# One triangular-inverse chain for both chunks and both heads of block 2, in place of one chain per chunk

## The chip, the cores and the metric

The kernel runs on one core of a Trainium2 chip. Its engines work side by side, each through its own instructions in order: TensorE (PE, matrix products, with PEld for its weight loads), VectorE (DVE), ScalarE (ACT), GpSimd (POOL) and SyncE (SP), which issues the transfers. The metric is the time of one execution on the device, in microseconds, as the median of three runs. A profiled execution gives the trace from which the rows below are taken.

## The reference

Three transformer blocks follow each other on 256 tokens of width 2048. The change touches the recurrent branch of the second block (RWKV-7, 12 heads of 64, both directions of time), of which this is the core:

```python
for d in range(N_DIR):
    wd = -jax.nn.softplus(-(w0[d] + jnp.tanh(w_in[d]) @ w2[d])) - 0.5
    ad = jax.nn.sigmoid(a0[d] + a_in[d] @ a2[d])
    kd = k * (1.0 + (ad - 1.0) * k_a)
    y_sum = y_sum + rwkv7_scan(r4, wd4, kd4, v4, kk, ad4)   # d = 1: on flipped time
...
def step(S, inp):                                           # one token of rwkv7_scan
    r_t, d_t, k_t, v_t, kk_t, b_t = inp
    sa = jnp.einsum('bhij,bhj->bhi', S, -kk_t)
    S = S * d_t[:, :, None, :] + sa[..., None] * b_t[:, :, None, :] + v_t[..., None] * k_t[:, :, None, :]
    return S, jnp.einsum('bhij,bhj->bhi', S, r_t)
```

The state S is 64 x 64 per head. The kernel computes the scan in two chunks of 128 tokens, and for that it needs, for each chunk and head, the inverse of a 128 x 128 matrix: the identity plus a strictly lower part for one direction of time and a strictly upper part for the other.

## The kernel before

The program is written in Python, one function per stage, and a scheduler of the tile layer then sets each engine's order. So the instructions of stages that don't depend on each other stand mixed in an engine's order, and each engine goes through its own order without overtaking.

Block 2's mixing stage (`block2_mix`) runs six pairs of heads (`rwkv_pair(p)`, p = 0 to 5). In a pair, `shift_mix` makes keys, receptances and values by weight products; `rwkv_setup` and `rwkv_rates` make the decay factors of both directions; `fill()` does cross-attention (pairs 0 and 1) or a group of output products (2 to 5). Then, for each of the two chunks n, `rwkv_gram` makes "gram" tiles: per head seven planes of 128 x 128, copied out of PSUM under a triangular mask (L1272). Plane 0 holds both strict triangles, of which the inverse is wanted. `rwkv_scan` uses the other planes and the inverses for both directions, and `gqa_pair` follows with the pair's share of windowed attention.

`pair_inverse` inverts the matrices of one chunk, two heads at a time. It keeps two tiles, "ylo" and "yup", with two planes for each head: the inverse of the lower part with the transpose of that of the upper part, and the reverse. It doubles the block size level by level, from 1 to 64:

- level 0: the matrix and its transpose (L1342) are put under a level mask into the identity;
- levels 1 to 6: `pt`, the matrix by the lower plane (L1349); z, a copy of the upper planes (L1351), and t, a copy of `pt` out of PSUM (L1352), both by ScalarE; the lower and upper product (L1358, L1359); and the puts of their results into the planes under the level's mask (L1339).

A put is a `copy_predicated` of VectorE. It takes its source in order and writes it "zipped": runs of s = 2^level adjacent elements fall by turns into the one plane and the other:

```python
return bass.AP(v.tensor, v.offset, [v.ap[0], (2 * s, 64 // s), (P + s, 2), (1, s)])
```

The chain of chunk 0 works in PSUM lane A and that of chunk 1 in lane B, two banks each, so both can be under way at once. A lane also names its own buffers: "yloA" and "yloB". Block 1 uses the same function with one head.

The weight products of the whole kernel (`wtiles`, L335 and L339) use a high and a low part of each weight, which ScalarE and VectorE split ahead (L290, L291). They depend on little and so stand between the chain's products as filler: where the chain's next product must wait, TensorE is busy with them as long as there are any before it in its order.

Of the kernel before, what the change touches and what calls it, by code (L numbers as in the profile page):

```python
# [18 lines left out]
P = 128  # L19
T = 256  # L20
# [184 lines left out]
class Core:  # L205
# [821 lines left out]
    def block2_mix(self):  # L1027
# [5 lines left out]
        if "lev" not in self.c:  # L1033
            self.load_mask(self.const, "lev")
# [93 lines left out]
    def rwkv_pair(self, p, finish, fill):  # L1128
# [8 lines left out]
        preps, grams, ups = [], [], []  # L1137
# [9 lines left out]
        fill()  # L1147
        for n in range(2):
            with self.on("AB"[n]):
                g, up = self.rwkv_gram(n, preps)  # L1150
                grams.append(g)
                ups.append(up)
        for d in range(2):
            with self.on("AB"[d]):
                self.rwkv_scan(d, preps[d], grams, ups, vt, ysum)
        return lambda: self.rwkv_end(p, r, v, [q[2] for q in preps], ysum)

    def rwkv_end(self, p, r, v, kds, ysum):
        rg = self.wtile(self.ins["w2_rg"][p], self.hs)
        gate = self.bp.tile([P, T], F32, name=self.uid("rgate"), tag="rgate", bufs=2)  # L1160
        self.wmul(gate, rg, self.rstd)
        self.twice_silu(gate, self.bp.tile([P, T], F32, name=self.uid("rgt"), tag="rgt", bufs=1))
        with self.on("A"):
            self.rwkv_finish(p, r, v, kds, ysum, gate)
# [25 lines left out]
    def rwkv_finish(self, p, r, v, kds, ysum, g):  # L1190
# [18 lines left out]
        y = self.tmp("ry")  # L1209
# [45 lines left out]
    def rwkv_gram(self, n, dirs):  # L1255
        nc, c = self.nc, self.c
        ch = slice(n * P, n * P + P)
        grams = []
        for h in range(2):
            g = self.tmp("gram", (P, 7, P), bufs=2)  # L1260
            nc.gpsimd.memset(g, 0.0)
            grams.append(g)
        for d, (ar, bk, _, _) in enumerate(dirs):
# [5 lines left out]
            for g, pg in zip(grams, pgs):  # L1269
                for j in range(2):  # L1270
                    dst = g[:, 2 + 3 * d:4 + 3 * d] if j else g[:, 0:2 + 3 * d:1 + 3 * d]
                    nc.vector.copy_predicated(dst, mask, pg[:, j * T:j * T + T].rearrange("p (a t) -> p a t", a=2))  # L1272
        _, up = self.pair_inverse([g[:, 0] for g in grams])
        return grams, up

    def rwkv_scan(self, d, prep, grams, ups, vt, ysum):
# [4 lines left out]
        g = {(n, h, j): grams[n][h][:, j + 3 * d] for n in range(2) for h in range(2) for j in (1, 2, 3)}  # L1281
        ys = [[up[:, h, 1 - d] for h in range(2)] for up in ups]
        state = None
        for n in (first, second):
# [25 lines left out]
            if state is None:  # L1310
# [10 lines left out]
                for hs in HALF:  # L1321
                    nc.scalar.activation(state[hs, hs], pS[hs, hs], AF.Copy, scale=carry[hs])

# [373 lines left out]
```

## Time and profile before

| What | Value |
|---|---|
| median of 3 runs | 3600.6 us (3599.87 to 3605.9) |
| the profiled execution: time, span | 3601.28 us, 3599.5 us |
| TensorE, VectorE, ScalarE, GpSimd busy | 98%, 74%, 50%, 2% of the span |
| granted clock of TensorE, mean | 0.993 |
| chain products L1349 in block 2, first to last | from 1503.8 to 2095.9 us of the span |
| pair 3, from its first gram product to the end of its scans | from 1839.6 to 1892.9 us |

The span runs from the first to the last instruction; the time also has what lies around it. TensorE is nearly always busy, so the table's shares say little on a stage: one has to look at the stretches in which the chains run. Matrix products overlap, and their ends are modelled; the distance from start to start says more than a busy time. A product of 32-bit operands is two instructions in a row.

### The profile page before, as it was taken

The numbers are of one execution on the slowest core, as the hardware profiler recorded it, in microseconds if no ns is written. First come the engines' busy times: TensorE is split into PE (matmuls) and PEld (weight loads), VectorE is DVE, ScalarE is ACT, GpSimd is POOL, SyncE is SP. The second block draws the span as 40 slices with busy tenths as digits, with TensorE's granted clock in tenths as the row PEclk, the third lists the DMA queues.
The fourth block names the chain that finished last, engine by engine and source line by source line (L and its number), as shares of the span: only waits on it lengthen the run. The fifth ranks groups of instructions, "written<-read, shape, count | busy, mean of one in ns | idle before, by whom it ended". The sixth has DMA issues, their size and how long they took to land.

```text
span 3599.5 us, 59008 instructions
## 1 busy us (share of the span) xinstructions
PE 3514.4 (98%) x22656; PEld 3144.6 (87%) x22656; DVE 2662.4 (74%) x5500; ACT 1814.2 (50%) x3138; POOL 61.6 (2%) x190
## 2 busy tenths in 40 slices
PE   8889999999999999999999999999999999999998
PEld 6889998999999998888888888889888888888887
DVE  7788988776767668877878867778776666666666
ACT  4156665544545455555555545554444544444444
POOL 0000000000000000000000000000000000000000
PEclk9989999999999999999999999999999999999999
DMA  8965777656666557332234336574445545555554
GB/s 337 351 237 200 263 266 265 225 208 219 222 206 231 188 181 239 133 125 107 103 115 138 125 117 213 188 253 170 172 168 185 187 176 202 176 198 180 195 184 144
DMA packets 128011, 700.99 MB, mean 195 GB/s; under 512 B 14449, under 2 KB 39537, under 8 KB 58865
## 3 DMA queue, kind: packets, MB, share of 16 engines
q1 hardware_dynamic: 127730, 697.22, 55.0%
q8 instruction: 179, 2.93, 0.3%
q14 instruction: 102, 0.84, 0.1%
HBM read 686.94 MB, written 10.22 MB: 194 GB/s over the span
## 4 chain that ended last, share of the span: by engine, by line
PE 86%; DVE 8%; ACT 3%; DMA 1%; issue 1%; SPq 0%; ACTq 0%; DVEq 0%
PE acc L335 36%; PE acc L339 18%; PE acc L309 12%; PE acc L313 6%; DVE wlo L291 2%; DVE ada L496 2%; PE acc L1349 1%; ACT whi L290 1%; PE acc L1358 1%; PE acc L1359 1%; PE acc L623 1%; PE acc L990 1%; PE acc L374 1%; DMA ada<-in_w_ada 1%; PE acc L369 1%
## 5 line engine op out<-in xcount | busy, mean ns | idle before, releaser
L290 ACT CAST whi<-wraw 128x1024 fp32r<-128x1024 f32 x1118 | 1096.1, 982 | 1199.0 <-PE acc L335 706.9
L291 DVE TENSOR_TENSOR wlo<-wraw,whi 128x1024 fp32r<-128x1024 f32 x1118 | 1272.7, 1140 | 514.5 <-ACT whi L290 412.4
L335 PE MATMUL acc<-a,whi 128*128 128x512 f32 x5888 | 1535.6, 396 | 6.7 <-ACT gt L346 1.7
L335 PEld LDWEIGHTS acc<-a,whi 128*128 128x128 f32 x5888 | 1043.1, 188 | 197.9 <-issue 5.4
L339 PEld LDWEIGHTS acc<-a,wlo 128*128 128x128 f32 x5888 | 816.9, 188 | 75.4 <-issue 4.0
L339 PE MATMUL acc<-a,wlo 128*128 128x256 f32 x5888 | 848.7, 282 | 0.0
L309 PE MATMUL acc<-a,whi 128*128 128x258 f32 (+1 forms) x3872 | 523.5, 284 | 0.2 <-ACT whi L290 0.2
L309 PEld LDWEIGHTS acc<-a,whi 128*128 128x128 f32 x3872 | 485.4, 190 | 0.9 <-ACT whi L290 0.4
L313 PE MATMUL acc<-a,wlo 128*128 128x258 f32 (+1 forms) x1936 | 282.8, 284 | 0.0
L313 PEld LDWEIGHTS acc<-a,wlo 128*128 128x128 f32 x1936 | 252.2, 190 | 0.3 <-issue 0.3
L496 DVE SCALAR_TENSOR_TENSOR ada<-ada,csilu 128x2048 f32<-128x2048 f32 x96 | 219.4, 2285 | 9.0 <-DMA ada<-in_w_ada 8.7
L1339 DVE COPY_PREDICATED ylo<-m_lev,acc 128x128 f32<-128x128 uint8 x200 | 82.8, 416 | 48.6 <-PE acc L1359 47.6
L369 PE MATMUL acc<-whi,a 128*128 128x256 f32 x416 | 108.3, 290 | 1.8 <-ACT whi L290 1.8
L1351 ACT COPY z<-yup 128x128 f32<-128x128 f32 x192 | 56.1, 300 | 102.5 <-DVE yup L1339 59.9
L370 PE MATMUL acc<-whi,a 128*128 128x256 f32 x416 | 107.6, 288 | 0.0
L356 DVE TENSOR_TENSOR x<-acc,x 128x256 f32<-128x256 f32 x128 | 54.2, 424 | 51.7 <-PE acc L339 51.7
L347 DVE TENSOR_TENSOR gt<-acc,gt 128x256 f32<-128x256 f32 x214 | 89.0, 418 | 3.5 <-ACT gt L346 2.9
L346 ACT COPY gt<-acc 128x256 f32<-128x256 f32 x214 | 78.0, 364 | 17.6 <-PE acc L339 17.6
L369 PEld LDWEIGHTS acc<-whi,a 128*128 128x128 f32 x416 | 80.0, 192 | 2.8 <-ACT whi L290 2.0
L370 PEld LDWEIGHTS acc<-whi,a 128*128 128x128 f32 x416 | 79.9, 192 | 0.0
L1359 PE MATMUL acc<-z,t 128*128 128x128 f32 x384 | 72.4, 278 | 0.2 <-ACT t L1352 0.2
L1358 PE MATMUL acc<-t,z 128*128 128x128 f32 x336 | 69.2, 290 | 2.0 <-ACT t L1352 2.0
(514 smaller groups left out, 3372.7 us busy)
## 6 DMA issues: line engine op xcount, KB each, us to landing
wraw<-in_w_up SPq DMA_DIRECT2D x132, 1024.0 KB, 4.8
ada<-in_w_ada SPq DMA_DIRECT2D x96, 1024.0 KB, 5.2
wraw<-in_w_down SPq DMA_DIRECT2D x128, 704.0 KB, 4.1
wraw<-in_w_out SPq DMA_DIRECT2D x48, 1024.0 KB, 4.9
wraw<-in_w_mg SPq DMA_DIRECT2D x48, 1024.0 KB, 4.9
wraw<-in_w_gate SPq DMA_DIRECT2D x44, 1024.0 KB, 4.7
wraw<-in_w_rs SPq DMA_DIRECT2D x20, 1024.0 KB, 5.1
wrow<-in_w_rows SPq DMA_DIRECT2D x16, 1024.0 KB, 8.5
```

The costliest lines, as they stand in the source:

```text
L290: nc.scalar.copy(hi[:, :m], raw[:, a:a + m])
L291: nc.vector.tensor_sub(lo[:, :m], raw[:, a:a + m], hi[:, :m].bitcast(F32))
L309: nc.tensor.matmul(acc, w, m, start=(n == 0), stop=False)
L313: nc.tensor.matmul(acc, lo[:, k % 8 * P:k % 8 * P + P], hs[k - c * kt][0], start=False, stop=(n == last))
L335: nc.tensor.matmul(both, hi[:, k % 8 * P:k % 8 * P + P], hs[k - c * kt][2], start=(n == 0), stop=False)
L339: nc.tensor.matmul(acc[:, :T], lo[:, k % 8 * P:k % 8 * P + P], hs[k - c * kt][0], start=False, stop=(n == last))
L347: self.nc.vector.tensor_add(out, acc[0], out)
L369: self.nc.tensor.matmul(accs[t], hs[k][0][:, ts], hi[:, ws], start=(k == 0), stop=False)
L370: self.nc.tensor.matmul(accs[t], hs[k][1][:, ts], hi[:, ws], start=False, stop=False)
L496: nc.vector.scalar_tensor_tensor(raw, raw, 1.0, self.cs, op0=ALU.mult, op1=ALU.mult, accum_out=self.mod[:, n:n + 1])
L1358: nc.tensor.matmul(pu4[:, 0, h], z2[:, h], t1[:, h], start=True, stop=True)
L1359: nc.tensor.matmul(pu4[:, 1, h], t1[:, h], z2[:, h], start=True, stop=True)
```

## The change

`group_inverse` takes the place of the two calls of `pair_inverse` in block 2. One tile "gram" (7 planes x 4 matrices x 128) holds both chunks and both heads. The planes of ylo and yup stand outside and the four matrices inside, so that one instruction handles all four: per level one z, one t, one lower and one upper put, each of 512 columns. The lower and the upper products go into PSUM tiles of their own, `pl` and `pu`, all lower ones first. `load_levels` loads the level masks a second time, at the start of block 2, and casts them into four copies side by side. One memset clears the gram tile. Two scratch tiles ("rgt", "ry") now come from the ring "gt" of six buffers.

```diff
-        if "lev" not in self.c:
-            self.load_mask(self.const, "lev")
+        self.lev4 = self.load_levels(bp, 4)
...
+        grams = self.bp.tile([P, 7, 4, P], F32, name=self.uid("gram"), tag="gram", bufs=1)
+        nc.gpsimd.memset(grams, 0.0)
         for n in range(2):
             with self.on("AB"[n]):
-                g, up = self.rwkv_gram(n, preps)
-                grams.append(g)
-                ups.append(up)
+                self.rwkv_gram(n, preps, grams)
+        _, up = self.group_inverse(grams[:, 0], self.lev4, "AB")
         for d in range(2):
             with self.on("AB"[d]):
-                self.rwkv_scan(d, preps[d], grams, ups, vt, ysum)
+                self.rwkv_scan(d, preps[d], grams, up, vt, ysum)
...
-        self.twice_silu(gate, self.bp.tile([P, T], F32, name=self.uid("rgt"), tag="rgt", bufs=1))
+        self.twice_silu(gate, self.gt())
...
-        y = self.tmp("ry")
+        y = self.gt()
...
-        _, up = self.pair_inverse([g[:, 0] for g in grams])
-        return grams, up
...
+    def load_levels(self, pool, copies):
+        lo, w = CCOL["lev"]
+        t = pool.tile([P, 7, copies, P], U8, name=f"m_lev{copies}")
+        f = self.wp.tile([P, 2048], F32, name=self.uid("mraw"), tag="wraw", bufs=WRAW)
+        self.nc.sync.dma_start(f[:, :w], self.ins["consts"][:, lo:lo + w])
+        f3 = f[:, :w].rearrange("p (l t) -> p l t", l=7)
+        for j in range(copies):
+            self.nc.vector.tensor_copy(t[:, :, j], f3)
+        return t.rearrange("p l h t -> p l (h t)")
+
+    def group_inverse(self, mats, lev, lanes, lower=False):
+        nc = self.nc
+        H = mats.shape[1]
+        with self.on(lanes[0]):
+            lo, up = (self.tmp(n, (P, 2, H, P)) for n in ("ylo", "yup"))
+            t1, z2 = self.tmp("t1", (P, H, P)), self.tmp("z2", (P, H, P))
...
+        def zipped(t, l, h=0, n=H):
+            v, s = t[:, 0, h], 1 << l
+            return bass.AP(v.tensor, v.offset, [v.ap[0], (2 * s, n * 64 // s), (H * P + s, 2), (1, s)])
...
+        put = lambda t, l, src: nc.vector.copy_predicated(zipped(t, l), flat(lev[:, l], l), flat(src, l))
+        heads = [slice(h * P, h * P + P) for h in range(H)]
+        one = lambda t: t.rearrange("p h t -> p (h t)")
+        pn = bank(lanes[0])
+        for h, hc in enumerate(heads):
+            nc.tensor.transpose(pn[:, hc], mats[:, h], self.ident)
+        put(up, 0, one(mats))
+        put(lo, 0, pn)
+        for l in range(1, 7):
+            pt = bank(lanes[1])
+            for h, hc in enumerate(heads):
+                nc.tensor.matmul(flat(pt[:, hc], l), mats[:, h], zipped(lo, l, h, 1), start=True, stop=True)
+            nc.scalar.copy(flat(one(z2), l), zipped(up, l))
+            nc.scalar.copy(one(t1), pt)
+            both = l < 6 or lower
+            pl = bank(lanes[0]) if both else None
+            if both:
+                for h, hc in enumerate(heads):
+                    nc.tensor.matmul(pl[:, hc], z2[:, h], t1[:, h], start=True, stop=True)
+                put(lo, l, pl)
+            pu = bank(lanes[1])
+            for h, hc in enumerate(heads):
+                nc.tensor.matmul(pu[:, hc], t1[:, h], z2[:, h], start=True, stop=True)
+            put(up, l, pu)
+        return lo, up
```

In the changed kernel the transposes are L1352, the products `pt`, `pl` and `pu` are L1358, L1365 and L1369, z and t are L1359 and L1360, the puts L1347, and the gram products L1262.

Where the program stands on the engines is set by the scheduler. First TensorE in pair 3, ahead of the first chain product. Before, from the first transpose (L1342; `acc_20502` is filler, 20154 and 20156 are the two heads of chunk 0):

```order
L1342 MATMUL acc_20184<-c_ident,gram_20154 128x128
L335 MATMUL acc_20502<-a_15632,whi_20494 128x512
L335 MATMUL acc_20502<-a_15635,whi_20494 128x512
L1342 MATMUL acc_20184<-c_ident,gram_20156 128x128
L335 MATMUL acc_20502<-a_15638,whi_20494 128x512
L335 MATMUL acc_20502<-a_15641,whi_20494 128x512
L335 MATMUL acc_20502<-a_15644,whi_20494 128x512
L1349 MATMUL acc_20191<-ylo_20178,gram_20154 128x128
L335 MATMUL acc_20502<-a_15647,whi_20494 128x512
L1349 MATMUL acc_20191<-ylo_20178,gram_20156 128x128
```

The changed kernel there, from the last gram products (chunk 1, backward) on; ahead of them stand two transposes with two L335 before the first, one between them and five behind:

```order
L1262 MATMUL acc_19944<-ar_19644,bk_19645 128x256 x2
L1262 MATMUL acc_19945<-ar_19644,bk_19645 128x256 x2
L1352 MATMUL acc_19960<-c_ident,gram_19912 128x128
L339 MATMUL acc_20177<-a_15632,wlo_20170 128x256
...
L1352 MATMUL acc_19960<-c_ident,gram_19912 128x128
L339 MATMUL acc_20177<-a_15644,wlo_20170 128x256
...
L335 MATMUL acc_20177<-a_15656,whi_20173 128x512
...
L335 MATMUL acc_20177<-a_15668,whi_20173 128x512
L1358 MATMUL acc_19967<-ylo_19954,gram_19912 128x128 x4
```

Left out are two, then three more L339 of the first and second four and three L335 of the five. The first chain product has moved behind all gram products of the pair, and eight L339 and five L335 stand behind the last of them.

Then the levels on TensorE, pair 3, before (chunk 0's chain reads t_3520, chunk 1's t_3543):

```order
L1349 MATMUL acc_20236<-ylo_20178,gram_20154 128x128
L1358 MATMUL acc_20320<-t_3543_20303,z_3544_20304 128x128
L1349 MATMUL acc_20236<-ylo_20178,gram_20156 128x128
L1359 MATMUL acc_20320<-z_3544_20304,t_3543_20303 128x128
L1358 MATMUL acc_20320<-t_3543_20303,z_3544_20304 128x128
L1359 MATMUL acc_20320<-z_3544_20304,t_3543_20303 128x128
L1358 MATMUL acc_20242<-t_3520_20180,z_3521_20181 128x128
L1359 MATMUL acc_20242<-z_3521_20181,t_3520_20180 128x128
```

and in the changed kernel, levels 2 and 3:

```order
L1365 MATMUL acc_19993<-t_3479_19956,z_3480_19957 128x128 x4
L1369 MATMUL acc_19999<-z_3480_19957,t_3479_19956 128x128 x4
L1358 MATMUL acc_20005<-ylo_19954,gram_19912 128x128 x4
L335 MATMUL acc_20306<-a_15635,whi_20298 128x512
L335 MATMUL acc_20306<-a_15638,whi_20298 128x512
L1452 MATMUL acc_20216<-gt_20210,c_perm 128x256
L335 MATMUL acc_20306<-a_15641,whi_20298 128x512
L335 MATMUL acc_20306<-a_15644,whi_20298 128x512
L1365 MATMUL acc_20012<-t_3479_19956,z_3480_19957 128x128 x4
```

Where one chain's products stood among the other's, four products of one chain now stand in a run, with filler only between `pt` and `pl`. Between these two stand, in pair 3, at level 1 three L335 and one L339; at level 2 seven L339 and one L335; at level 3 the rows above; at level 4 two small products (L1499) and three score products of 64 rows (L1468), with a fourth ahead of the next `pt`; at level 5 three L335 and two L339; at level 6, ahead of `pu`, two L1282 of the scan, three L339 and four transposes.

Last VectorE, pair 3 of the changed kernel, at the first puts and at level 4:

```order
L1268 COPY_PREDICATED gram_19912<-m_tri_b,acc_19944 128x2x128 x2
L1268 COPY_PREDICATED gram_19912<-m_tri_b,acc_19945 128x2x128 x2
L1347 COPY_PREDICATED yup_19955<-m_lev_15744,gram_19912 128x256x2
L1347 COPY_PREDICATED ylo_19954<-m_lev_15744,acc_19960 128x256x2
L291 TENSOR_TENSOR wlo_20303<-wraw_20296,whi_20302 128x1024
...
L1347 COPY_PREDICATED yup_19955<-m_lev_15744,acc_20018 128x32x2x8
L1501 TENSOR_SCALAR hm_20225<-acc_20222 128x4
...
L1504 TENSOR_SCALAR rq_20227<-rq_20227 128x4
L1474 SCALAR_TENSOR_TENSOR sm_20247<-acc_20241,rq_20227,c_win 128x256
L1347 COPY_PREDICATED ylo_19954<-m_lev_15744,acc_20031 128x16x2x16
```

Before, eight puts of 128 columns took the place of the first two here, in groups of four for each chunk, and the small operations of the attention's scale (L1452 to L1455 before, L1501 to L1504 now, twelve in all) had four puts of chunk 1 among them.

## Rows read from the trace of the kernel before

**Rows 1.** The page: busy time by engine, and the chain that ended last.

```profile
PE 3514.4 (98%) x22656; PEld 3144.6 (87%) x22656; DVE 2662.4 (74%) x5500; ACT 1814.2 (50%) x3138; POOL 61.6 (2%) x190
PE 86%; DVE 8%; ACT 3%; DMA 1%; issue 1%; SPq 0%; ACTq 0%; DVEq 0%
```

**Rows 2.** A window of pair 3: length, busy time by engine (instructions), clock, DMA.

```profile
1839.00:1860.00 21.00, 19.63 (x110) 14.38 (x109) 17.70 (x44) 7.83 (x18) 0.00 (x0) 1.00 0.34 118
```

**Rows 3.** TensorE's timeline, filler: start us, length us, engine, line, operation, tiles, count.

```profile
1487.53 2.02 PE L335 MATMUL acc<-a,whi 128*128 128x512 f32 x8
1489.38 1.10 PE L339 MATMUL acc<-a,wlo 128*128 128x256 f32 x8
```

**Rows 4.** TensorE's timeline, pair 3; in brackets idle before, and what ended it.

```profile
1845.90 2.74 PE L1267 MATMUL acc<-ar,bk 64*128 64x256 f32 x16
...
1849.38 0.30 PE L1342 MATMUL acc<-c_ident,gram 128*128 128x128 f32 x1 [0.75 <-DVE gram L1272]
...
1850.02 0.94 PE L335 MATMUL acc<-a,whi 128*128 128x512 f32 x3
1851.15 0.51 PE L1349 MATMUL acc<-ylo,gram 128*128 128x128 f32 x2 [0.20 <-DVE ylo L1339]
1851.40 0.49 PE L335 MATMUL acc<-a,whi 128*128 128x512 f32 x1
1852.27 0.51 PE L1349 MATMUL acc<-ylo,gram 128*128 128x128 f32 x2 [0.39 <-DVE ylo L1339]
...
1854.34 0.39 PE L1358 MATMUL acc<-t,z 128*128 128x128 f32 x2
1854.57 0.39 PE L1359 MATMUL acc<-z,t 128*128 128x128 f32 x2
...
1861.61 0.72 PE L335 MATMUL acc<-a,whi 128*128 128x512 f32 x2
1862.39 0.49 PE L1349 MATMUL acc<-ylo,gram 128*128 128x128 f32 x2
...
1882.62 0.94 PE L335 MATMUL acc<-a,whi 128*128 128x512 f32 x3
1883.68 0.66 PE L1296 MATMUL acc<-xw,yup 128*128 128x64 f32 x4
```

**Rows 5.** VectorE's timeline in pair 3, level 0 and level 1.

```profile
1848.80 1.11 DVE L1272 COPY_PREDICATED gram<-m_tri_b,acc 128x256 f32<-128x256 uint8 x3
...
1851.27 0.95 DVE L1339 COPY_PREDICATED ylo<-m_lev,acc 128x128 f32<-128x128 uint8 x1
1851.84 1.65 DVE L1272 COPY_PREDICATED gram<-m_tri_f,acc 128x256 f32<-128x256 uint8 x4
...
1855.24 0.47 DVE L1339 COPY_PREDICATED yup<-m_lev,acc 128x128 f32<-128x128 uint8 x1
```

**Rows 6.** Line 1339, all instructions: count, shortest/median/longest ns, first and last start.

```profile
L1339 DVE COPY_PREDICATED yup<-m_lev,acc x192: 283/296/504, 239.4 to 2098.2; 128x128 f32<-128x128 uint8 x192
L1339 DVE COPY_PREDICATED yup<-m_lev,gram x24: 714/741/971, 1502.3 to 2074.6; 128x128 f32<-128x128 uint8 x24
```

**Rows 7.** Groups by line: count, busy us, mean ns, idle before and releaser.

```profile
L1272 DVE COPY_PREDICATED gram<-m_tri_b,acc 128x256 f32<-128x256 uint8 x48 | 19.0, 441 | 1.5 <-PE acc L1267 1.5
L1468 ACT COPY sm<-acc 128x512 f32<-128x512 f32 x16 | 9.4, 585 | 8.7 <-PE acc L1466 8.6
```

**Rows 8.** VectorE's timeline, pair 3: first and last operation of the attention's scale.

```profile
1878.67 0.16 DVE L1452 TENSOR_SCALAR hm<-acc 128x4 f32<-128x4 f32 x1
...
1882.65 0.17 DVE L1455 TENSOR_SCALAR rq<-rq 128x4 f32<-128x4 f32 x1
```

**Rows 9.** ScalarE's and TensorE's timelines at the blocks' seam; the mask's cast.

```profile
1431.89 1.05 ACT L290 CAST whi<-wraw 128x1024 fp32r<-128x1024 f32 x1 [1.53 <-DMA wraw<-in_w_rs]
...
1437.19 2.70 PE L335 MATMUL acc<-a,whi 128*128 128x512 f32 x11
...
L242 DVE CAST m_lev<-mraw x1: 621/621/621, 82.0 to 82.0; 128x896 uint8<-128x896 f32 x1
```

More of the change, by code (lines that the diff above doesn't have):

```diff
@@ L1136, in rwkv_pair @@
             kk, vt, ysum = self.rwkv_setup(p, k, v)
-        preps, grams, ups = [], [], []
+        preps = []
         pls = [[], []]
@@ L1253, in rwkv_rates, with rwkv_gram @@
         return ar, bk, kd, carry
-    def rwkv_gram(self, n, dirs):
+    def rwkv_gram(self, n, dirs, grams):
         nc, c = self.nc, self.c
         ch = slice(n * P, n * P + P)
[L1258 to L1262, printed above, removed]
         for d, (ar, bk, _, _) in enumerate(dirs):
@@ L1268, in rwkv_gram @@
             mask = c["tri_b" if d else "tri_f"].rearrange("p (a t) -> p a t", a=2)
-            for g, pg in zip(grams, pgs):
+            for h, pg in enumerate(pgs):
+                g = grams[:, :, 2 * n + h]
                 for j in range(2):
@@ L1272, in rwkv_gram, with rwkv_scan @@
                     nc.vector.copy_predicated(dst, mask, pg[:, j * T:j * T + T].rearrange("p (a t) -> p a t", a=2))
[L1273 to L1276 removed]
+    def rwkv_scan(self, d, prep, grams, up, vt, ysum):
         nc = self.nc
@@ L1280, in rwkv_scan @@
         first, second = (1, 0) if d else (0, 1)
-        g = {(n, h, j): grams[n][h][:, j + 3 * d] for n in range(2) for h in range(2) for j in (1, 2, 3)}
-        ys = [[up[:, h, 1 - d] for h in range(2)] for up in ups]
+        g = {(n, h, j): grams[:, j + 3 * d, 2 * n + h] for n in range(2) for h in range(2) for j in (1, 2, 3)}
+        ys = [[up[:, 1 - d, 2 * n + h] for h in range(2)] for n in range(2)]
         state = None
@@ new lines, in group_inverse, with bank @@
+    def group_inverse(self, mats, lev, lanes, lower=False):
[4 more added lines that the diff above has]
+            t1, z2 = self.tmp("t1", (P, H, P)), self.tmp("z2", (P, H, P))
+        for t in (lo, up):
+            nc.gpsimd.tensor_copy(t.rearrange("p y h t -> p (y h) t"),
+                                  self.ident.unsqueeze(1).to_broadcast([P, 2 * H, P]))
+        def zipped(t, l, h=0, n=H):
+            v, s = t[:, 0, h], 1 << l
+            return bass.AP(v.tensor, v.offset, [v.ap[0], (2 * s, n * 64 // s), (H * P + s, 2), (1, s)])
+        def bank(lane):
+            with self.on(lane):
+                return self.psum(False)[:, :H * P]
+        flat = lambda ap, l: ap.rearrange("p (m e s) -> p m e s", e=2, s=1 << l)
+        put = lambda t, l, src: nc.vector.copy_predicated(zipped(t, l), flat(lev[:, l], l), flat(src, l))
[23 more added lines that the diff above has]
+        return lo, up
```

## The prediction

> **What bounds the kernel now.** I read the page first. TensorE is busy 98% of the span, VectorE 74%, ScalarE 50%, GpSimd 2%, and 86% of the chain that ended last is TensorE [rows 1]. So a microsecond counts only where TensorE stands still or is given more to do. The matrix products of the changed kernel are the same ones: per pair four transposes and 68 chain products, before and after. What can change is how long TensorE waits for the chain, in six places, one per pair.
>
> Then the windows of pair 3, whose stretch from the first gram product to the end of the scans runs from 1839 to 1893 us. In the first 21 us TensorE is idle 1.37 us at full granted clock, while VectorE is busy 17.7 [rows 2]. Pairs 2 to 5 stand in the same order, so pair 3 speaks for them; pairs 0 and 1 have other filler and nearly the same places.
>
> Then TensorE's timeline there. It is in-order, and between chain products stand weight products as filler. Filler back to back starts every 0.23 us (L335: 8 in 1.85 us) and about 0.12 us (L339: 8 in 1.10 us with the last one's tail) [rows 3]; chain products start 0.23 us apart, and a result is out 0.39 us after its start [rows 4]. Against these prices the losses in pair 3 are: 0.75 us ahead of the first transpose; three L335 (0.69) that fill 1.13 us before the first L1349, so 0.44; one L335 (0.23) that fills 0.87 before the second, so 0.64; two L335 (0.46) that fill 0.78, so 0.32; and, at the scan, three L335 that fill 1.06, so 0.37 [rows 4]. That is 1.8 us at the front (level 0), 0.3 in the levels, 0.4 in the scans: 2.5 us per pair, 15 us in all six. More than this, and some small change of switching, the change cannot take away.
>
> **The price of a put.** VectorE's masked write into the zipped planes (L1339) takes 0.30 us for one matrix of 128 columns in most levels and 0.74 at level 0 [rows 6]; at level 1, 0.47, and at level 0 they follow each other every 0.57, so that 0.17 of each is overlapped [rows 5]. The run of adjacent elements is 1 at level 0, 2 at level 1, 4 or more later: the price is by short runs, not by the instruction. A masked copy of 256 columns with long runs takes 0.44 [rows 7], 0.14 more than 128 columns. So my estimates for four matrices in one put: 0.30 + 3 x 0.14 = 0.73 us at levels 2 to 6; 4 x 0.30 + 0.17 = 1.37 at level 1; 4 x 0.57 + 0.17 = 2.45 at level 0. No row shows a hop between planes of 513 elements (it was 129), so for levels 0 and 1 the lower bound is 0.73, as if short runs cost nothing, and the upper the figures given. I take the upper, nearest to the level-0 row, which is the same write with fewer runs.
>
> **The change, part by part.**
>
> *Level 0.* Before, chain 0 begins when chunk 0's grams are masked, at 1849.91 [rows 5], and its first product needs one head's two puts. Now all four matrices of both chunks must be masked, and then two puts of 2.45 us run one after the other. From 1848.63, where TensorE ran dry, the new order gives it, up to the first chain product: 13 L335 (3.0), 8 L339 (0.95), 4 transposes (0.9) and 4 gram products (8 in 2.74 us [rows 4], so 1.4): 6.25 us, plus some 0.4 of waiting at the first two transposes (two L335 now stand ahead of them). It is ready at 1855.3. VectorE masks the forward half of chunk 1 in 1.65 us [rows 5], to 1851.5. The backward half waits for the four gram products, which TensorE reaches at 1851.3 and ends at 1852.7; the last copy is done at 1853.2. Then up to 1855.5 the first put holds VectorE, and the second is done at 1857.95. TensorE waits from 1855.3 to 1858.0, 2.7 us. Front: 0.4 + 2.7 = 3.1 for 1.8 before, **+1.3 us** a pair. With puts at the lower bound there is no wait: 0.4 for 1.8, -1.4.
>
> *Between pl and the next pt.* The split of the PSUM tile lets the lower put run beside the upper products. From the last pl product TensorE has 0.23 + 4 x 0.23 = 1.15 us of work; the put needs 0.39 + 0.73 + about 0.1, a tenth more. Such tenths I take as equal on both sides. At level 1 it needs 0.39 + 1.37 + 0.1, so 0.7 us of wait.
>
> *Between pt and pl.* The chain now has nothing beside it but filler. z and t are 512 columns each; a ScalarE copy of 512 columns takes 0.585 [rows 7]. Upper put, z, then t end about 2.2 us after the first pt product, which covers 0.92 itself: 1.25 us of filler is wanted, and the order has 0.81, 1.06, 1.41, 1.3, 0.93 and 1.7 in the six levels. At level 1 z is done early and 0.1 is short; at level 2 the level-1 puts are late and 0.35 is short; at level 5, 0.3. Sum 0.75.
>
> *VectorE's queue at level 4.* The order puts the attention's 12 small operations and a 128x256 one ahead of the lower put. In the trace such a run takes 4.15 us with four puts and a sum among it [rows 8], about 3.0 without. The put starts some 1.0 us late; a leftover score product covers half: 0.5 us.
>
> Levels: 0.7 + 0.75 + 0.5 = 1.95 for 0.3 before, **+1.6**; if everything were covered, -0.3.
>
> *What comes back.* Both scan directions now start together and fill each other's gaps, so I count the scan's 0.37 as gone. The gram products stand in five groups instead of six, and chain products in runs of four. No row prices a switch alone; it is between nothing and 1.0 us per pair, and I take 0.5. **-0.9**.
>
> *Edits costed at nothing.* The removed instructions on VectorE (52 puts become 13) and ScalarE (36 copies become 12) are off the path here: their engines have idle time in this stretch. The one big memset and the copies of the identity run on GpSimd, 2% busy [rows 1], after the previous pair's scans and some 50 us ahead of use; uncovered they would cost their length, some 3.4 us a pair (four memsets). The two tiles that move to the "gt" ring share six buffers whose other users are done within a few us; uncovered, one transfer each, some 2 us. The new mask is one more load of 0.46 MB ahead of block 2's first weights and four casts of 0.62 us [rows 9] at the seam of the blocks. The first weights were cast from 1431.89 and first used three L335 after 1437.19, at 1437.9 [rows 9]: some 4.9 us of cover after the cast, against a load that is about 3 us later. Uncovered: 2.5 us once.
>
> **Sum.** 1.3 + 1.6 - 0.9 = +2.0 us per pair, +12 in six. The profiled execution took 3601.3 us with a span of 3599.5, 0.7 above the median of 3600.6; its own time plus 12 gives 3613, against the median 3612.6. I say **3612 us**.
>
> **The rivals.** A change under 0.2%, 7 us, is no more than a measurement of this kernel can tell from none.
>
> *A. As above*, 3612. For it: puts priced by runs, and an order whose filler ahead of the first product ends 2.7 us early. Chance 0.42; it decides only while the two level-0 puts together are longer than some 2.2 us.
>
> *B. The level-0 put is cheap with the longer hop.* Then the front is -1.4 and the pair -1.4 + 1.6 - 0.9 = -0.7: 3597. Against it speaks that the price falls only with run length in the rows. [...] Chance 0.18.
>
> *C. Faster.* The one chain is covered everywhere: front -1.4, levels -0.3, the rest -0.9, so -2.6 per pair, 3585. It needs cheap short runs and, in each level, filler that is longer than the order shows. For it: ScalarE and VectorE lose two thirds of the instructions, so everything queued behind them comes earlier. [...] Chance 0.10.
>
> *D. Much slower.* Every level waits as level 4 does, because attention work, weight splits and casts of 1 us stand between the puts in the same queues, and no second chain is there to take TensorE's time: 0.7 us more in each of six levels, +4 a pair, 3636. Chance 0.10.
>
> *E. No change.* The waits are as small as before and only elsewhere: 3601. For it: equal products, and only 15 us of waits to move. Chance 0.20.
>
> Faster by over 0.2%: C and the low end of B, 0.14. Slower: D and most of A, 0.46. Within: 0.40. Case A alone is 3606 to 3619, by the bounds of the levels and the switching. The range takes in B and stops short of C and D, 2 in 10 together: 3590 to 3628.
>
> **What would show it.** In pair 3 after: the first L1358 group ahead of which TensorE idles 2 us or more, released by the lower plane's put; that put at 2.2 to 2.5 us for level 0, 1.3 to 1.4 for level 1, 0.7 later; a wait of about 0.7 ahead of the second L1358 group. Wrong would be: level-0 puts near 1 us (B), no wait ahead of the first group (B, C), waits ahead of every L1365 group (D). TensorE's products must be as many as before, and the seam at 1430 to 1450 without a new wait; a wait there of over 1 us would be a price that I set at nothing.

## The result: slower, 3626.8 us

| | median us | runs | range us |
|---|---|---|---|
| before, in the first comparison | 3600.23 | 4 | 3596.29 to 3605.90 |
| changed | 3626.82 | 4 | 3623.09 to 3628.99 |

The ratio is 1.0076, with a 95% interval of 1.0064 to 1.0088: 26.6 us slower. That is the forecast side, and 3626.8 lies just inside the forecast range (3590 to 3628), but it is more than twice the 12 us of the sum.

The page of the changed kernel, to hold against [rows 1]: as many products on TensorE, fewer operations on the other engines, and yet more of the chain on VectorE (10% for 8).

```profile
PE 3515.8 (97%) x22656; PEld 3145.2 (87%) x22656; DVE 2664.3 (74%) x5270; ACT 1790.5 (49%) x2994; POOL 58.2 (2%) x160
PE 83%; DVE 10%; ACT 3%; issue 2%; DMA 1%; SPq 0%; ACTq 0%; DVEq 0%
```

One full period, from the first gram product of a pair to that of the next, holds all work of a pair. Windows of pair 3 before (columns as in [rows 2]: length, busy time by engine, clock, DMA):

```profile
1839.62:1947.14 107.52, 105.82 (x656) 88.65 (x655) 86.39 (x237) 56.54 (x128) 6.41 (x16) 1.00 0.34 116
```

and of the changed kernel: pair 2, pair 3, 4 us around the first chain product of each, and the 2 us behind that of pair 3.

```profile
1729.21:1840.37 111.16, 105.82 (x655) 88.42 (x655) 85.65 (x198) 52.54 (x105) 6.07 (x11) 1.00 0.33 112
1840.37:1952.87 112.50, 107.18 (x655) 89.73 (x655) 85.63 (x198) 52.54 (x105) 6.07 (x11) 0.98 0.33 110
1754.00:1758.00 4.00, 2.30 (x15) 2.03 (x16) 2.70 (x2) 1.01 (x3) 0.00 (x0) 1.00 0.19 25
1866.00:1870.00 4.00, 3.11 (x11) 2.87 (x12) 1.89 (x2) 0.59 (x1) 0.00 (x0) 0.59 0.26 47
1867.00:1869.00 2.00, 2.00 (x9) 2.00 (x10) 0.89 (x1) 0.00 (x0) 0.00 (x0) 0.50 0.29 41
```

Read them as length less busy. TensorE stood idle 1.70 us in the period of before and 5.32 in pair 3 after: 3.62 more. Its busy time also grew by 1.36 for the same products, with a granted clock of 0.98: from 1867 to 1869 the clock stood at 0.50 of full. In pair 2 the same wait left it at 1.00 and the products took 105.82. Together +5.0 us in pair 3.

Where the idle time stands is in TensorE's timeline of pair 3 (start, length, what; in brackets idle before and its releaser), beside [rows 4]. A count is of instructions, two for a chain or gram product and one for a transpose or a filler product:

```profile
1857.95 0.30 PE L1352 MATMUL acc<-c_ident,gram 128*128 128x128 f32 x1 [0.50 <-DVE gram L1268]
...
1861.35 0.33 PE L1352 MATMUL acc<-c_ident,gram 128*128 128x128 f32 x1 [0.32 <-DVE gram L1268]
...
1866.89 2.08 PE L1358 MATMUL acc<-ylo,gram 128*128 128x128 f32 x8 [2.92 <-DVE ylo L1347]
1868.62 1.63 PE L335 MATMUL acc<-a,whi 128*128 128x512 f32 x3
1870.04 0.33 PE L339 MATMUL acc<-a,wlo 128*128 128x256 f32 x1
1870.21 1.05 PE L1365 MATMUL acc<-t,z 128*128 128x128 f32 x8
...
1872.63 1.16 PE L1358 MATMUL acc<-ylo,gram 128*128 128x128 f32 x8 [0.48 <-DVE ylo L1347]
...
1886.65 1.16 PE L1358 MATMUL acc<-ylo,gram 128*128 128x128 f32 x8 [0.20 <-DVE ylo L1347]
...
1893.15 0.44 PE L1515 MATMUL acc<-c_ident,sm 128*128 128x128 f32 x2 [0.45 <-DVE sm L1513]
```

With 0.41 ahead of the next pair's first gram product (released by VectorE's L1251) these are 5.28 of the 5.32. The same place in pair 2:

```profile
1755.70 1.23 PE L1358 MATMUL acc<-ylo,gram 128*128 128x128 f32 x8 [2.92 <-DVE ylo L1347]
...
1757.61 1.16 PE L1365 MATMUL acc<-t,z 128*128 128x128 f32 x8
```

In pair 2, at full clock, the first chain products and the same four filler products go from 1755.70 to 1757.61, 1.91 us; in pair 3 from 1866.89 to 1870.21, 3.32; in pairs 4 and 5 it is 3.36 and 3.33, and the clock stands at 0.50 in the 2 us behind each of the three waits. So the halved clock costs 1.4 us behind the wait, in pairs 3 to 5. Pairs 0 and 1, with other filler, wait 3.05 and 2.64 us ahead of their first chain products, also at full clock (1.00 in the 2 us behind them); pairs 2 to 5 wait 2.92.

VectorE's timeline shows what was waited for; the puts are L1347:

```profile
1862.19 2.44 DVE L1347 COPY_PREDICATED yup<-m_lev,gram 128x512 f32<-128x512 uint8 x1
1864.27 2.56 DVE L1347 COPY_PREDICATED ylo<-m_lev,acc 128x512 f32<-128x512 uint8 x1
...
1871.30 1.28 DVE L1347 COPY_PREDICATED ylo<-m_lev,acc 128x512 f32<-128x512 uint8 x1 [3.42 <-PE acc L1365]
...
1876.10 0.73 DVE L1347 COPY_PREDICATED ylo<-m_lev,acc 128x512 f32<-128x512 uint8 x1 [0.16 <-PE acc L1365]
```

Level 0, 1 and 2: 2.44, 1.28, 0.73 us, near the estimates of 2.45, 1.37 and 0.73.

Last, the seam of blocks 1 and 2. Rows of filler on TensorE, before; the first and the last correspond to the first and the last of the changed kernel:

```profile
1430.55 2.01 PE L335 MATMUL acc<-a,whi 128*128 128x512 f32 x8
...
1434.40 2.01 PE L335 MATMUL acc<-a,whi 128*128 128x512 f32 x8
...
1449.53 2.01 PE L335 MATMUL acc<-a,whi 128*128 128x512 f32 x8
```

and the changed kernel's, with the wait between them, and below it all four casts of the mask on VectorE (count, shortest/median/longest ns, first and last start):

```profile
1426.46 2.01 PE L335 MATMUL acc<-a,whi 128*128 128x512 f32 x8
...
1432.47 3.16 PE L335 MATMUL acc<-a,whi 128*128 128x512 f32 x8 [2.00 <-ACT whi L290]
...
1449.22 2.01 PE L335 MATMUL acc<-a,whi 128*128 128x512 f32 x8
```

```profile
L1325 DVE CAST m_lev<-mraw x4: 1082/1085/1087, 1427.3 to 1431.3; 128x896 uint8<-128x896 f32 x4
```

Ahead of the seam this execution was 4.1 us earlier than that of before, for reasons that lie before block 2, and behind the seam 0.3 us earlier: 3.8 lost, 2.0 as a wait for block 2's first weights and about 1.1 in eight products at a lowered clock (3.16 us for 2.01, with 0.62 granted from 1432.40 to 1435.70). From the first gram product of pair 0 (1493.20 before, 1492.45 after) to corresponding rows behind the sixth pair (2171.66 before, 2193.64 after) the pairs take 22.7 us more, 3.8 each. The 3.8 at the seam and the 22.7 in the pairs, 26.5 us in these two traces, stand beside the 26.6 of the medians.

### The profile page after: what moved, and what is told of

It reads as the page before. It is cut to its first block, busy times and chain, and to the rows that moved or that the text cites. A ratio compares the mean times of both kernels' runs of the same rounds, so it can differ in the third digit from the quotient of the medians.

```text
span 3621.2 us, 58466 instructions
## 1 busy us (share of the span) xinstructions
PE 3515.8 (97%) x22656; PEld 3145.2 (87%) x22656; DVE 2664.3 (74%) x5270; ACT 1790.5 (49%) x2994; POOL 58.2 (2%) x160
## 3 DMA queue, kind: packets, MB, share of 16 engines
q8 instruction: 178, 2.92, 0.3%
## 4 chain that ended last, share of the span: by engine, by line
PE 83%; DVE 10%; ACT 3%; issue 2%; DMA 1%; SPq 0%; ACTq 0%; DVEq 0%
PE acc L335 35%; PE acc L339 18%; PE acc L309 11%; PE acc L313 6%; DVE wlo L291 2%; DVE ada L496 2%; ACT whi L290 1%; PE acc L623 1%; PE acc L1358 1%; PE acc L990 1%; PE acc L374 1%; PE acc L369 1%; PE acc L370 1%; DMA ada<-in_w_ada 1%; DVE ylo L1347 1%
## 5 line engine op out<-in xcount | busy, mean ns | idle before, releaser
L291 DVE TENSOR_TENSOR wlo<-wraw,whi 128x1024 fp32r<-128x1024 f32 x1118 | 1275.5, 1143 | 514.8 <-ACT whi L290 414.4
L335 PE MATMUL acc<-a,whi 128*128 128x512 f32 x5888 | 1534.8, 396 | 9.1 <-DVE a L391 2.2
L335 PEld LDWEIGHTS acc<-a,whi 128*128 128x128 f32 x5888 | 1044.6, 188 | 204.9 <-issue 8.6
L339 PEld LDWEIGHTS acc<-a,wlo 128*128 128x128 f32 x5888 | 816.4, 188 | 72.8 <-issue 0.7
L339 PE MATMUL acc<-a,wlo 128*128 128x256 f32 x5888 | 840.6, 281 | 0.0
L356 DVE TENSOR_TENSOR x<-acc,x 128x256 f32<-128x256 f32 x128 | 54.2, 424 | 51.6 <-PE acc L339 51.5
L374 PE MATMUL acc<-wlo,a 128*128 128x256 f32 x416 | 70.1, 287 | 0.4 <-DVE wlo L291 0.4
L1358 PE MATMUL acc<-ylo,gram 128*128 128x128 f32 x288 | 44.7, 300 | 20.7 <-DVE ylo L1347 17.6
L357 DVE TENSOR_TENSOR x<-acc,x 128x256 f32<-128x256 f32 x144 | 60.9, 423 | 3.7
L1358 PEld LDWEIGHTS acc<-ylo,gram 128*128 128x128 f32 x288 | 37.5, 202 | 28.8 <-DVE ylo L1347 23.0
```

The source lines that it names most:

```text
L291: nc.vector.tensor_sub(lo[:, :m], raw[:, a:a + m], hi[:, :m].bitcast(F32))
L335: nc.tensor.matmul(both, hi[:, k % 8 * P:k % 8 * P + P], hs[k - c * kt][2], start=(n == 0), stop=False)
L339: nc.tensor.matmul(acc[:, :T], lo[:, k % 8 * P:k % 8 * P + P], hs[k - c * kt][0], start=False, stop=(n == last))
L374: self.nc.tensor.matmul(accs[t], hs[k][0][:, ts], lo[:, ws], start=False, stop=(k == nk - 1))
L1358: nc.tensor.matmul(flat(pt[:, hc], l), mats[:, h], zipped(lo, l, h, 1), start=True, stop=True)
```

## The experiments

All medians stand beside runs of the kernel before on the same chip (3598.9 to 3600.3). Where kernels of different chips are compared, the differences below are taken of what each has over before on its own chip.

**1. Two wide chains.** One `group_inverse` for each chunk:

```diff
-                self.rwkv_gram(n, preps, grams)
-        _, up = self.group_inverse(grams[:, 0], self.lev4, "AB")
+                self.rwkv_gram(n, preps, grams)
+                ups.append(self.group_inverse(grams[:, 0, 2 * n:2 * n + 2], self.lev4, "AB"[n] * 2)[1])
```

> The changed kernel, but with one chain per chunk again: group_inverse is called for the two matrices of chunk 0 right after its grams, in lane A, and for those of chunk 1 in lane B. All else stays: the one gram tile, the planes outside, the products in tiles of their own, the second mask load. Theory (the merging of the chunks costs: TensorE must wait for all grams and for 5 us of level-0 puts, and then runs at half clock): the six pairs come back to what they were, about 22 us less, and the 4 us at the seam of the blocks stay: 3605 us, and no wait of more than 1 us ahead of a first chain product. Rival (the layout with far planes, or the split tiles, or the two small tiles in the other ring cost): little comes back, 3620 us or more.

Measured 3620.79 us, ratio 1.0060 (1.0047 to 1.0073). The theory fell: only 6 us came back. Its timeline of pair 3 still waits for puts, and for the attention:

```profile
1862.48 0.75 PE L1358 MATMUL acc<-ylo,gram 128*128 128x128 f32 x4 [1.10 <-DVE ylo L1347]
...
1869.82 1.19 PE L1358 MATMUL acc<-ylo,gram 128*128 128x128 f32 x8 [0.83 <-DVE ylo L1347]
...
1909.78 0.70 PE L1515 MATMUL acc<-c_ident,sm 128*128 128x128 f32 x4 [1.14 <-DVE sm L1513]
```

So the merging of the chunks is not by itself what costs.

**2. The lower put first.**

```diff
-        put(up, 0, one(mats))
         put(lo, 0, pn)
+        put(up, 0, one(mats))
```

> The changed kernel with the two level-0 puts in the other order, the lower plane first. The first chain product needs only the lower one; z needs the upper one. Theory (the series of the two puts is the wait): the first product starts about 2 us earlier and ScalarE's copy z is waited for instead, about 0.6 us less per pair where the clock stayed up and 2.1 where it fell, about 8 us in six pairs: 3618 us. Rival (the waits in the levels, where one chain has nothing beside it, are the cost): the wait only moves from the first product to the second group, 3627 us.

Measured 3625.15 us, 1.0073 (1.0059 to 1.0087): 1.7 less, nearer to the rival. The first wait fell, but a wait for ScalarE's copies took its place (z waits for the upper put, and t, which the row names, is copied behind z), and another came ahead of the attention's transposes:

```profile
1869.18 1.23 PE L1358 MATMUL acc<-ylo,gram 128*128 128x128 f32 x8 [1.33 <-DVE ylo L1347]
1872.69 1.16 PE L1365 MATMUL acc<-t,z 128*128 128x128 f32 x8 [1.35 <-ACT t L1360]
...
1911.01 0.44 PE L1515 MATMUL acc<-c_ident,sm 128*128 128x128 f32 x2 [2.03 <-DVE sm L1513]
```

**3. Useless work in the wait.**

```diff
             pt = bank(lanes[1])
+            if l == 1:
+                for h in range(8):
+                    nc.tensor.matmul(pt[:, heads[h % 4]], self.ident, up[:, 0, h % 4], start=True, stop=True)
```

> The changed kernel with useless work: eight products of 128 columns (1.8 us of TensorE per pair) that need only the upper level-0 put and whose result is overwritten by the first chain products. They fall in the 2.9 us in which TensorE stands still. Theory (the granted clock falls to half because TensorE stands still that long, and the 1.6 us lost behind the wait in pairs 3 to 5 are that clock's): the clock stays at 1.00 there, and the added work makes the kernel 5 to 9 us faster: 3618 to 3622 us. Rival (the slow products behind the wait have another cause, or the clock falls anyway): not faster, 3627 us, and up to 11 us more where the added products are not hidden.

Measured 3620.63 us, 1.0058 (1.0045 to 1.0070): 6.2 less, with 48 more products. Pair 3, with the added ones as L1359 and the first chain products as L1361, and the clock in the window around them:

```profile
1868.44 2.02 PE L1359 MATMUL acc<-yup,c_ident 128*128 128x128 f32 x16 [1.46 <-DVE yup L1347]
1870.61 1.23 PE L1361 MATMUL acc<-ylo,gram 128*128 128x128 f32 x8
```

```profile
1867.00:1874.00 7.00, 5.42 (x41) 4.99 (x42) 4.89 (x4) 1.26 (x2) 0.00 (x0) 1.00 0.20 43
```

The first chain products take 1.23 us as in pair 2, not 2.08, and the clock stays at 1.00, here and over the periods of pairs 2 and 3 below. So the clock does not fall behind a wait of 1.46 us that ends in the useless products. Not all of the 6 us is the clock's, though. The periods of pairs 2 and 3:

```profile
1733.80:1844.10 110.30, 106.99 (x670) 90.33 (x670) 86.12 (x198) 52.29 (x105) 6.03 (x11) 1.00 0.33 113
1844.10:1954.28 110.18, 106.85 (x671) 90.31 (x671) 86.13 (x198) 52.21 (x105) 6.03 (x11) 1.00 0.33 113
```

Pair 3 takes 2.3 us less than in the changed kernel, but pair 2, where the clock had not fallen, also takes 0.9 less: the order behind the added products is another, and the waits of 0.20 and 0.45 us are gone. That leaves about 1.4 us for the clock in pair 3, and, as an estimate, as much in pairs 4 and 5: some 4 of the 6 us.

**4. No second load of the mask.**

```diff
-        f = self.wp.tile([P, 2048], F32, name=self.uid("mraw"), tag="wraw", bufs=WRAW)
-        self.nc.sync.dma_start(f[:, :w], self.ins["consts"][:, lo:lo + w])
-        f3 = f[:, :w].rearrange("p (l t) -> p l t", l=7)
+        f3 = self.c["lev"].rearrange("p (l t) -> p l t", l=7)
         for j in range(copies):
-            self.nc.vector.tensor_copy(t[:, :, j], f3)
+            self.nc.gpsimd.tensor_copy(t[:, :, j], f3)
```

> The changed kernel without the second load of the level mask: its four copies are made by GpSimd from the mask that block 1 already holds, so no transfer, no buffer of the weights' ring and no VectorE cast at the seam. Theory (the load and its casts hold up the first weights of block 2, 2 us of wait and then half clock): 4 us less, 3623 us, and the wait for the first weights at the start of block 2 is gone. Rival (the seam's loss comes from elsewhere, as from the buffers that the blocks change): 3627 us with the wait still there.

Measured 3626.62 us, 1.0077 (1.0064 to 1.0089): no gain in the median. The wait for the first weights is gone in the trace; one of 1.02 us ahead of L438, for VectorE's L430, stands a little later, and the pairs of this execution took some 3 us more, with the clock lowered in pairs 1 and 2 too (0.76 from 1645 to 1649 us, 0.83 from 1755 to 1765). The wait itself is the load's: all six traces with the load have it (1.67 to 2.14 us), none of the eight without it. The lowered clock behind it shows in two of the six (the next eight L335 take 3.16 us in the changed kernel and 3.61 in 3, 2.12 or 2.13 in the others), and a wait at L438 of about 1.1 us also in 5, where the seam is that of before. In the median the seam's price stays unproven (and see 9).

**5. Before, with the two ring edits alone.**

```diff
-        self.twice_silu(gate, self.bp.tile([P, T], F32, name=self.uid("rgt"), tag="rgt", bufs=1))
+        self.twice_silu(gate, self.gt())
...
-        y = self.tmp("ry")
+        y = self.gt()
```

> The kernel before with one part of the change alone: the two small tiles (rgt, ry) come from the ring of six buffers. Theory (these two edits cost nothing, as forecast): 3600 us. Rival (the shared ring delays the pair's end and is what stays, some 2.5 us per pair, after the chains were separated again): 3612 us or more.

Measured 3603.08 us, 1.0008 (1.0000 to 1.0017). Neither end is excluded: nothing, or some 6 us. The trace shows the 0.42 us ahead of the first gram product that the changed kernel has and before has not, in pairs 2 to 5, 1.7 us in all; the wait ahead of the first transpose falls from 0.75 to 0.50 in return. Pair 3's period is 108.10 us for 107.52, with less idle (1.54 for 1.70) and more busy time. What makes the busy time longer was not traced.

**6. The old chains in the new frame.** `pair_inverse` again for each chunk, on the one gram tile, no second load:

```diff
-        self.lev4 = self.load_levels(bp, 4)
...
-        _, up = self.group_inverse(grams[:, 0], self.lev4, "AB")
+                ups.append(self.pair_inverse([grams[:, 0, 2 * n + h] for h in range(2)])[1])
```

> The changed kernel with the old chains: one gram tile, one memset and the shared ring as in the changed kernel, but pair_inverse for each chunk, one put for each matrix, both products in one PSUM tile, and the old mask without a second load. Theory (what the separated wide chains still had over the kernel before, 3 us at the seam and about 2.5 per pair, comes from the wide instructions, the split tiles and the load): 3601 us. Rival (it comes from the frame: one gram tile, one memset, the ring): 3612 to 3616 us.

Measured 3609.27 us, 1.0029 (1.0018 to 1.0041), between the two. Ahead of its first chain products TensorE waits as in [rows 4]; what is new in pair 3's period is 1.18 us ahead of the attention's transposes, for VectorE's L1512 (1.2 to 1.6 in pairs 1 to 4, 5.2 in all), and 0.42 at the first gram product. So by the medians some 6 us beyond the ring come with the frame. Why the order puts the attention later there was not tried.

**7. A put twice.** One more `put(lo, 0, pn)` behind the two.

> The changed kernel with one suspected cost doubled: the lower level-0 put is written twice (same result). Theory (what VectorE does ahead of the first chain product is TensorE's wait, one for one): 2.4 us more per pair, and half clock behind the wait in more pairs: 3641 to 3646 us. Rival (the levels behind are what costs, and the front is half covered): 3632 us or less.

Measured 3639.59 us, 1.0113 (1.0100 to 1.0127): 14.1 more, 2.3 a pair, about the theory's 2.4 (the time is 1.4 us under its span) and far from the rival. Pair 3:

```profile
1882.06 2.04 PE L1359 MATMUL acc<-ylo,gram 128*128 128x128 f32 x8 [4.60 <-DVE ylo L1347]
```

The wait grew by 1.68: the third put takes 2.34 us and a weight split (L291) of 1.45 now stands ahead of it, but 1.9 us more of filler cover them. The clock now falls in pair 2 too (0.57 from 1765 to 1770 us), which is part of the price.

**8. Level 0 in two plain steps.**

```diff
-        put(up, 0, one(mats))
-        put(lo, 0, pn)
+        def put0(t, tmp, src):
+            v = t[:, 0, 0]
+            zv = bass.AP(v.tensor, v.offset, [v.ap[0], (P, H), (2, P // 2), (H * P + 1, 2)])
+            nc.vector.tensor_mul(one(tmp), src, lev[:, 0])
+            nc.vector.tensor_add(zv, tmp.rearrange("p h (m e) -> p h m e", e=2), zv)
+        put0(up, z2, one(mats))
+        put0(lo, t1, pn)
```

> The changed kernel with level 0 written in two plain steps in place of each predicated put: the matrices times the mask into a scratch tile (512 adjacent columns), then a sum of it with the planes, written zipped with the same far hop. Theory (the predicated write is dear at short runs, not the hop): product and sum some 0.7 us each, the level takes 2.8 instead of 4.9 us of VectorE, the wait ahead of the first product falls under 1 us and the clock stays up: 2 to 4 us less per pair, 3605 to 3613 us. Rival (each write of single elements with a far hop costs the same, predicated or not): the sum takes 2.4 us, the level 6 us, 3633 us or more.

Measured 3603.30 us, 1.0014 (1.0005 to 1.0023): 22.2 of the 26.6 us are back. VectorE, then TensorE in pair 3:

```profile
1855.65 0.68 DVE L1356 TENSOR_TENSOR z<-gram,m_lev 128x512 f32<-128x512 f32 x1
1856.25 0.68 DVE L1356 TENSOR_TENSOR t<-acc,m_lev 128x512 f32<-128x512 f32 x1
1856.85 1.13 DVE L1357 TENSOR_TENSOR yup<-z,yup 128x512 f32<-128x512 f32 x1
1857.82 1.15 DVE L1357 TENSOR_TENSOR ylo<-t,ylo 128x512 f32<-128x512 f32 x1
```

```profile
1856.12 2.01 PE L335 MATMUL acc<-a,whi 128*128 128x512 f32 x8
1857.96 0.64 PE L339 MATMUL acc<-a,wlo 128*128 128x256 f32 x4
1859.12 1.20 PE L1363 MATMUL acc<-ylo,gram 128*128 128x128 f32 x8 [0.53 <-DVE ylo L1357]
```

The level now takes 3.3 us of VectorE (1855.65 to 1858.97) for 4.6 (1862.19 to 1866.83). The rest of the gain has two sources: the order puts eight L335 and four L339 ahead of the first product where five L335 stood, 1.2 us more cover, and the clock stays up (1.00 from 1858 to 1861 us). The period is 108.28 us with 2.56 idle.

**9. The same, without the second load.** Edits 8 and 4 together.

> The changed kernel with level 0 in two plain steps and the mask copied by GpSimd from block 1's, without a second load. Theory (the load costs some 2 to 3 us at the seam, and in the earlier run without it the clock's falls behind the waits hid that): with those waits gone the gain shows, 3600 to 3601 us. Rival (nothing is lost at the seam in the median): 3603 us.

Measured 3602.68 us, 1.0012 (1.0003 to 1.0021): 1.2 less than 8, not told from nothing.

**10. Lower plane first, level 1's lower put split.** As 9, and:

```diff
-        put0(up, z2, one(mats))
         put0(lo, t1, pn)
+        put0(up, z2, one(mats))
...
-                put(lo, l, pl)
+                for g in range(2 if l == 1 else 1):
+                    w = H // 2 if l == 1 else H
+                    c = slice(g * w * P, (g * w + w) * P)
+                    nc.vector.copy_predicated(zipped(lo, l, g * w, w), flat(lev[:, l, c], l), flat(pl[:, c], l))
```

> As the kernel with level 0 in two steps and no second load, and two more edits: at level 0 the lower plane is written first, and at level 1 the lower put is split by chunk, so that the next products of chunk 0 need only the first half. Theory (what is left are TensorE's waits of 0.5 us ahead of the first chain product and 0.5 at level 2, both behind VectorE): some 0.9 us less per pair, 3595 to 3597 us, under the kernel before. Rival (the wait goes to the attention's transposes or to a copy by ScalarE): 3600 us or more.

Measured 3596.19 us, 0.9994 (0.9985 to 1.0002): 6.5 under 9, 29.9 under the changed kernel, and level with before, no proven gain on it. The two edits were not tried apart. The period, 107.07 us with 1.54 idle, and the wait that is left ahead of the first chain product:

```profile
1827.81:1934.88 107.07, 105.53 (x655) 88.51 (x655) 82.63 (x201) 52.47 (x105) 5.93 (x11) 1.00 0.34 116
```

```profile
1852.25 1.20 PE L1361 MATMUL acc<-ylo,gram 128*128 128x128 f32 x8 [0.18 <-DVE ylo L1355]
```

**11. Before, with level 0 in two steps**, in `pair_inverse` of both blocks (two products with the mask and one sum for each tile).

> The kernel before with level 0 in two plain steps (in blocks 1 and 2), nothing else. Theory (there the two chains cover the dear puts of each other, only 1.0 us per pair is lost at the front, and two steps for two matrices take VectorE hardly less than four puts): 3597 to 3601 us. Rival (the dear put is the bound there too): 1 us less per pair and some in block 1, 3592 us.

Measured 3596.91 us, 0.9994 (0.9985 to 1.0003), no proven change. In its trace the waits of 0.20 and 0.39 us ahead of the chain products in [rows 4] are gone, and of the front's waits only the 0.75 ahead of the first transpose is left. Pair 3's period:

```profile
1842.55:1948.98 106.43, 105.66 (x655) 89.62 (x654) 85.54 (x239) 56.50 (x128) 6.58 (x16) 1.00 0.34 117
```

That is 1.1 us less than before, the rival's price, and 0.6 less than the one chain has in 10. From the first gram product to behind the sixth pair this trace takes 5.7 us less than that of before, but it reaches block 2's first gram product 5.7 us later, after a lower granted clock from 400 to 800 us (0.97 for 1.00), in block 1, which the edit changes too. The mean clock of all its runs is lower as well, 0.990 to 0.992 for 0.991 to 0.994; why is not shown. The edit in block 2 alone was not tried.

**12. Two wide chains with level 0 in two steps**, the lower plane first, no second load.

> One wide chain for each chunk again, with level 0 in two plain steps (the lower plane first) and no second load. Theory (with the dear put gone, one chain for both chunks costs no more than two): 3600 to 3604 us, not below the one chain with the same two edits. Rival (one chain has nothing to fill its levels, and two have): 3597 us or less.

Measured 3614.83 us, 1.0048 (1.0035 to 1.0060): 12 slower than one chain in 9. It waits for the attention, in pair 3, and the clock falls behind that wait (eight L335 from 1903.70 take 2.95 us, the next eight 2.02); below the row, the periods of pairs 2 and 3:

```profile
1901.94 0.89 PE L1518 MATMUL acc<-c_ident,sm 128*128 128x128 f32 x4 [2.15 <-DVE sm L1516]
```

```profile
1728.06:1838.69 110.63, 107.40 (x655) 89.11 (x655) 87.46 (x215) 54.34 (x117) 6.41 (x13) 1.00 0.32 112
1838.69:1950.87 112.18, 108.97 (x655) 90.45 (x655) 87.53 (x215) 54.34 (x117) 6.42 (x13) 0.98 0.32 111
```

Against 9 (108.23 us in pair 2, 105.69 of them busy) pair 2 has 0.7 us more idle and 1.7 more busy time at full clock. What the longer busy time is was not traced.

## Why the prediction came out so

The direction and its mechanism held: case A, the wait ahead of the first L1358 group behind two level-0 puts in series. Experiments 7 and 8 show it, by dearer and by cheaper writing of level 0 with the chain left alone. The size lay above case A's own span of 3606 to 3619 and nearer to D, but not by D's mechanism: in pairs 2 to 5 no wait stands ahead of the L1365 groups (in pairs 0 and 1 one of 0.45 and 0.54 us). That the range holds it is partly luck, since what carried it there beyond case A are a clock and a seam that the sum left out. Term by term, in us, for pair 3:

| Term of the sum | forecast | measured |
|---|---|---|
| the two level-0 puts, each | 2.45 | 2.44 and 2.56 |
| wait ahead of the first chain product | 2.7 | 2.92 |
| waits at transposes | 0.4 | 0.50 + 0.32 |
| front before | 1.8 | 0.75 + 0.20 + 0.39 |
| front, change | +1.3 | +2.4 |
| level 2's first group | 0.7 | 0.48 |
| between pt and pl | 0.75 | no idle of note |
| level 4 | 0.5 | 0.20 |
| attention's transposes in level 6 | none | 0.45 |
| returned | -0.9 | none seen |
| first gram product | none | 0.41 |
| half clock behind the wait | none | 1.4 in pairs 3 to 5 |
| seam, once | nothing | 3.8 in the trace |

- **Put prices.** Right to about a tenth of a microsecond: at level 0 the put for four matrices took 2.44 us, some four times the 0.57 that a put for one took from start to start.
- **The front, mis-sized.** I had taken the loss of before as start distances over ideal prices, 1.8, which counts as loss what TensorE is busy with above those prices between products of two kinds; the idle time was 1.34. And the third transpose waits again. The step is the first term of the sum: +1.3 forecast, +2.4 measured.
- **"What comes back", wrong.** The -0.9 rested on 0.5 for fewer switches, for which no row spoke, and 0.37 in the scans. No such gain shows in the period: TensorE's busy time is 105.82 us in pair 3 before and in pair 2 after.
- **The clock, left out.** The sum carried waits at their length. Pairs 3 to 5 show that a wait of 2.92 us can cost 1.4 more than itself, and experiment 3 that the 1.4 goes when eight products shorten the wait to 1.46.
- **Edits costed at nothing.** The prediction saw 4.9 us of cover behind the cast of the first weights, as it took the L335 group at 1437.19 for the first that uses them. It is the one at 1434.40, behind the last three products of block 1's weights (as the one at 1432.47 in the changed kernel), and the cast ends at 1432.94: 1.5 us of cover. The load came about as late as forecast: SyncE issues it 3.4 us later, against the stream of products, than before (at 1426.10 for 1426.83, in an execution 4.1 us ahead), and TensorE waits 2.0. The mask's casts took 1.08 us each, not 0.62; they write into a tile of four copies. Experiments 4 and 9 took the wait away without a proven gain in the median, so 3.8 is the traces' figure alone. The ring edits and the frame were not free: experiment 6 has 10 us with the old chains (without the load).
- **The levels**, +1.6 forecast: 0.48, 0.20 and 0.45 for 0.15 before (at the attention's transposes), +1.0. The gaps between pt and pl were covered.
- **Rival B** was excluded by the 2.44 us, 4.8 ns for each of 512 columns. In experiment 8 the plain sum with the same hop, and one on a source as well, took 1.13 us, 2.2 ns each: here it is the predicated write that is dear, not the hop by itself.
- **Rival C** had the sign of what the chain can do once level 0 is cheap: experiment 10 is 29.9 us under the changed kernel, but only level with before.

After the result I blamed the merging of the chunks. Experiments 1 and 12 show that it isn't the merging by itself: separated chains are 6 us faster with the dear put, 12 slower without it. What costs in the changed kernel is the VectorE work that stands in series ahead of a TensorE product that has run out of filler; experiments 7 and 8 show this for level 0, though both also moved filler. Open: why the order puts the attention later in the frame of experiment 6, what lengthens TensorE's busy time in 5 and 12, and why the clock stayed up in pairs 0 to 2 of the same execution.

## What to carry to other kernels

When several small chains become one wide chain, add up the longest instructions that now stand in series ahead of its first consumer (here two puts of 2.44 and 2.56 us, and a wait of 2.92). The count of instructions saved on an engine that is not the bound did not make up for that here: VectorE had 230 fewer, and the kernel was 26.6 us slower. Price a masked, interleaved write by its run length (2.44, 1.28 and 0.73 us here for 512 columns in runs of 1, 2 and 4), and try a plain product and sum in its place where runs are single elements (level 0 took 3.3 us of VectorE so, for 4.6). Look at the granted clock behind a wait of TensorE: those of 2.92 us cost 1.4 more than their length here in pairs 3 to 5. And give the kernel before the same cheap step before calling the wide chain level with it: in the traces the narrow chains with two steps had the shortest pair (106.43 us, experiment 11).

## What the hardware showed that I had not expected

- The granted clock went to 0.50 behind a 2.92 us wait in pairs 3 to 5 and stayed at 1.00 behind the same wait in pair 2. With eight useless products in the wait it stayed at 1.00 in pairs 2 and 3, and the kernel was 6 us faster, by my estimate some 4 of them by the clock.
- The same zipped write of 512 single elements takes VectorE 2.44 us as a predicated copy and 1.13 as a sum with the planes it writes (1.8 with the product by the mask ahead of it, 0.68).
- The cast of 896 columns to bytes takes 0.62 us into adjacent places [rows 9] and 1.08 into every fourth block of 128.
